# Two-block hybrid layer on one core: forgetting attention summed by even and odd key blocks, the gated recurrence's decays as products, bias table and latent keys made in other stages

## The chip, the cores and the metric

One core of a Trainium2 chip runs the whole program in one launch. The metric is device time in microseconds (us), the median of three runs: 3874.92 before (3865.3 to 3883.36). Engines: TensorE (PE, with its weight loads as PEld), VectorE (DVE), ScalarE (ACT), GpSimd (POOL) and SyncE (SP), which issues all DMAs in order.

## The reference, cut to what matters

Two layers over 2048 tokens of width 1024, all in float32. The first has five branches (spatial gating, forgetting attention, mLSTM, RWKV-7, memory attention), the second a sparse latent attention and a gated recurrence (HGRN2). The change touches three of these:

```python
def forgetting_attention(q, k, v, f_logit, q_g, k_g):   # 4 heads of 64
    q, k = rms_norm(to_heads(q), q_g), rms_norm(to_heads(k), k_g)
    big_f = cumsum(log_sigmoid(f_logit))
    s = einsum("bthd,bshd->bhts", q, k) * scale + big_f[t] - big_f[s]
    return einsum("bhts,bshd->bthd", softmax(causal(s)), v)

def hgrn2(q, f_raw, v, lb):                              # 4 heads, keys and values of 128
    q = silu(q)
    f = lb + (1 - lb) * sigmoid(f_raw)
    k = 1 - f
    # o_t = sum over s <= t of  (q_t . k_s . prod of f over (s, t])  v_s,  chunk by chunk, with a state

def latent_attention(ql, c, bias):                       # c: 128-wide latent keys, rms-normed
    logits = ql @ c.T * scale + rel_bias[bucket(s - t)]  # on the 256 keys picked for each query
    return softmax(logits) @ c
```

## The kernel before

The program is written out flat, and a scheduler puts each engine's instructions in an order by program order and simulated time; on the chip every engine, and SP's queue of DMAs, runs its order as it stands. Pools of tiles are opened on a left and a right side of the memory. A stage on the left (projections: `proj_chunk`, `proj2_chunk`, `gates`) runs beside one on the right (the mixers), and a tile of a new pool waits for the old tiles that lay there. A product in float32 is two PE instructions (a transpose is one), and a projection is three products of single-pass parts (`mm3`, L310 to L316), 24 matmuls for a block of 128 rows and 256 columns.

**Forgetting attention** (`fox_pair`, L793; `attend_pair`, L591). Two heads and 128 queries at a time. For each head the scores of `ns` key blocks go from PE through a DVE copy that keeps the maximum into a tile P (three buffers), ACT takes the exponential in place, and DVE inverts the sum. Then, for both heads together, four 128x128 transposes (two key blocks of two heads) fill a PSUM bank, ACT copies it to PT, and PE sums values into `o`, head 0 into its partitions 0 to 63 and head 1 into 64 to 127, so neighbouring matmuls use different halves of the columns (L616 to L628). At the end one copy, one transpose and two scaled products (L635) give the rows. The "CAM" projections of the first layer come later in program order and fill PE. After the attention its right-hand pools are closed and those of the mixers are opened (L849 onward: `mlstm_setup`, `mem_load`, `sgu_setup`).

**Gated recurrence** (`hgrn_quarter`, L1959), 512 tokens at a time, after projections of 6, 6 and 4 blocks of tokens (`proj2_chunk`, part "hgrn"). The forget gate is stored as exp(-f_raw) (L1401). `hgrn_decays` makes log f with two logarithms on ACT and a subtraction on POOL, and 1 - k with an exponential. Per head, a scan on DVE (L1979) gives the running sum b of log f. The scores within 128 tokens are split by levels, 64, 32, 16, 8, 4, 2, 1 and 0: at level lv the pairs of (key in the first half, query in the second half of a span of 2 lv tokens) are the product of two arrays that carry the decay up to the middle:

```python
nc.gpsimd.tensor_tensor(out=both(e), in0=both(b), in1=ref, op=ALU.subtract)              # L1992
nc.scalar.activation(out=v(e, j), in_=v(e, j), func=ACT.Exp, scale=2.0 * j - 1.0)        # L1994, j = 0, 1
nc.vector.tensor_tensor(out=v(e, 0), in0=v(e, 0), in1=v(kk, 0), op=ALU.mult)             # L1995
nc.vector.tensor_tensor(out=v(e, 1), in0=v(e, 1), in1=v(q, 1), op=ALU.mult)              # L1996
```

Levels 64 to 16 use small matmuls (L2007), the others eight matmuls of 64x64 each (L2018), merged into `near` by a predicated copy (L2019). Every level is made from b, independently of the others. Then exp(b) and exp(b_last - b) give the queries and keys for the state (L2025 to L2032), the keys are transposed, and a loop over four chunks of 128 tokens (L2037 to L2062) loads values hgv (L2041), multiplies scores and values (L2045), adds the state's part (L2046), updates the state (L2049, L2051), norms and gates the rows.

**Latent attention's setup.** While the gates' projection (`gates`, L1439, weights from L298, blocks by fours) runs beside the last quarter, before its third part `dsa_setup` (L1559) makes the bias table: a small matmul gives 4 rows of 512 floats in 4 partitions (gv), and one DMA (L1585) writes each row 128 times to DRAM (gd, 1 MB); four loads with a skewed pattern (L1589) bring `rel`. Before the fourth part `dsa_keys` (L1593) loads, norms and transposes the latent keys in four parts. `attend` (L2237) then runs the sparse attention beside the last projections.

Of the kernel before, what the change touches and what calls it, by code (L numbers as in the profile page):

```python
# [20 lines left out]
T = 2048  # L21
# [9 lines left out]
def _consts():  # L31
# [559 lines left out]
def attend_pair(k, get_s, ns, V, sz, y, bufs=3):  # L591


    nc = k.nc
    L = ns * 128
    o = k.bank("o", 1, 256)
    rden, Ps = [], []
    for h in range(2):
# [16 lines left out]
        rden.append(rd)  # L615
        Ps.append(P)  # L616

    for j0 in range(0, ns, 2):
        n = min(2, ns - j0)
        tp = k.bank("tp")  # L620
        work = [(h, j) for j in range(j0, j0 + n) for h in range(2)]
        for i, (h, j) in enumerate(work):
            k.transpose(tp[:, 128 * i:128 * i + 128], Ps[h][:, 128 * j:128 * j + 128])
        PT = k.wk.tile([128, 512], F32, tag="PT", name="PT", bufs=3)
        k.evict(PT[:, 0:256 * n], tp[:, 0:256 * n], "a")
        for i, (h, j) in enumerate(work):
# [88 lines left out]
def fox_setup(k, q_g, k_g, f_b):  # L715
# [9 lines left out]
    k.fox_fb = k.row(f_b, 4, "fox_fb")  # L725
    k.fox_F = k.const.tile([128, NB, 4, 2], F32R, name="fox_F")
# [635 lines left out]
def proj2_chunk(k, S, slots, w, blocks, part):  # L1362
# [87 lines left out]
def lb_setup(k, lb_logits):  # L1450

    nc = k.nc
    k.lb = k.const.tile([128, 4], F32, name="lb")
# [10 lines left out]
    nc.vector.tensor_tensor(out=k.lb, in0=l[:, 0], in1=m, op=ALU.mult)  # L1464
# [94 lines left out]
def dsa_setup(k, w_uk, w_uv, kv_g, rel_bias):  # L1559
    nc = k.nc  # L1560
    k.w_uk = k.const.tile([128, 4, 128], F32, name="w_uk")
    nc.sync.dma_start(out=k.w_uk, in_=w_uk.rearrange("h d r -> d h r"))
    k.w_uv = k.const.tile([128, 4, 128], F32, name="w_uv")
    nc.sync.dma_start(out=k.w_uv, in_=w_uv.rearrange("h r v -> r h v"))
    k.kv_g = k.row(kv_g, 128, "kv_g")
    k.cT = k.const.tile([128, 2, T], F32R, name="cT")
    k.cM = k.const.tile([128, NB, 128], F32, name="cM")
    k.last64 = k.const.tile([128, 128], BF16, name="last64")
    t = k.wk.tile([128, 128], F32, tag="cn", name="cn", bufs=1)
    nc.sync.dma_start(out=t, in_=k.cd["last64"])  # L1570
    nc.vector.tensor_copy(out=k.last64, in_=t)

    oh = k.wk.tile([32, 511], F32, tag="oh", name="oh", bufs=1)
# [19 lines left out]
def dsa_keys(k, S, part):  # L1593
# [334 lines left out]
def hgrn_setup(k, norm_g):  # L1928
    nc = k.nc
    k.hg_next = []  # L1930
# [4 lines left out]
    k.h_reset = k.const_in("h_reset", [128, 512])  # L1935
# [3 lines left out]
    k.h_mask = k.const.tile([128, 5, 64], U8, name="h_mask")  # L1939
    t = k.wk.tile([128, 320], F32, tag="hgm", name="hgm", bufs=1)  # L1940
    nc.sync.dma_start(out=t, in_=k.cd["h_mask"])
    nc.vector.tensor_copy(out=k.h_mask.rearrange("p l t -> p (l t)"), in_=t)


def hgrn_decays(k, S, h, qt):

    nc = k.nc
    f2, b2 = (k.wk.tile([128, 2, 512], F32, tag="hg" + n, name="hg" + n) for n in ("f", "b"))
    nc.sync.dma_start(out=f2, in_=S["f"][128 * h:128 * h + 256, 512 * qt:512 * qt + 512].rearrange("(h p) t -> p h t", p=128))

    for j in range(2):
        nc.scalar.activation(out=b2[:, j], in_=f2[:, j], func=ACT.Ln, scale=k.lb[:, h + j:h + j + 1], bias=1.0)
# [347 lines left out]
```

## Time and profile before

| | us |
|---|---|
| median of three runs | 3874.92 |
| lowest, highest run | 3865.3, 3883.36 |
| the profiled execution's own time | 3866.28 |
| its span in the profile | 3864.1 |
| PE busy in the span | 3541.2 (92%) |
| PEld, DVE, ACT, POOL busy | 3280.1, 2537.0, 1532.7, 764.6 |

The profile is of one execution. A line like L1994 is the line of the kernel before. In rows of groups, "x192 | 68.7, 412" means 192 instructions, 68.7 us of busy time, 412 ns the mean of one, then the idle time of that engine just before them and who ended it. PE's busy time counts pipelined instructions once where they overlap. PEclk is the granted clock as a share of full speed.

### The profile page before, as it was taken

Reading aid. Unit: us, or ns where it says so; the run is one execution under the profiler, and the core shown is the slowest. Engines: PE = TensorE matmul, PEld = TensorE weight load, DVE = VectorE, ACT = ScalarE, POOL = GpSimd, SP = SyncE. Lnnn points to the kernel's source line nnn. Section 1 sums busy time; section 2 is a strip of 40 time slices with the busy share of each in tenths; the row PEclk is TensorE's granted clock in tenths of the full one; section 3 lists DMA queues with packets and bytes.
Section 4 is the critical chain, followed back from the end, with each engine's and each line's share of the span. In section 5 each row is a group of like instructions: output and inputs, shape, how many; then the busy total and the mean of one; then the engine's idle time right before and its main releaser. Section 6 shows DMA issues by size and latency. Waiting matters only on the chain. (4 is left out here: it accounts for less than half of the span.)

```text
span 3864.1 us, 75038 instructions
## 1 busy us (share of the span) xinstructions
PE 3541.2 (92%) x28525; PEld 3280.1 (85%) x28525; DVE 2537.0 (66%) x7303; ACT 1532.7 (40%) x3257; POOL 764.6 (20%) x686
## 2 busy tenths in 40 slices
PE   6899999999899999789999989889888839899997
PEld 5899989889789999668898989878888838899997
DVE  5477777775734434488655478799777847665675
ACT  3221221222534434444422356566454533443443
POOL 2322222333100000102200000022043423331121
PEclk8999999999999999769899999989999969999998
DMA  8674444445632533446877785774646446653433
GB/s 291 205 224 138 133 157 138 145 144 171 196 120 101 173 130 115 145 141 209 261 247 250 249 263 207 227 238 150 228 161 209 166 115 197 215 187 135 137 124 114
DMA packets 449539, 691.54 MB, mean 179 GB/s; under 512 B 80324, under 2 KB 368526, under 8 KB 410256
## 3 DMA queue, kind: packets, MB, share of 16 engines
q1 hardware_dynamic: 449168, 686.65, 53.9%
q8 instruction: 226, 3.70, 0.4%
q14 instruction: 145, 1.19, 0.1%
HBM read 453.84 MB, written 232.69 MB: 178 GB/s over the span
## 5 line engine op out<-in xcount | busy, mean ns | idle before, releaser
L314 PE MATMUL pj<-whi,slot 128*128 128x256 f32 (+3 forms) x3856 | 1123.8, 292 | 33.1 <-DVE po L178 16.2
L316 PE MATMUL pj<-whi,slot 128*128 128x256 f32 (+3 forms) x3856 | 1119.9, 291 | 2.6 <-DVE slot L271 2.6
L315 PE MATMUL pj<-wlo,slot 128*128 128x256 f32 (+3 forms) x3856 | 1114.6, 289 | 0.8 <-POOL wlo L302 0.8
L314 PEld LDWEIGHTS pj<-whi,slot 128*128 128x128 f32 x3856 | 742.9, 193 | 56.4 <-DVE po L178 16.8
L316 PEld LDWEIGHTS pj<-whi,slot 128*128 128x128 f32 x3856 | 741.4, 192 | 18.9 <-issue 9.0
L315 PEld LDWEIGHTS pj<-wlo,slot 128*128 128x128 f32 x3856 | 742.9, 193 | 14.3 <-issue 7.7
L314 PE MATMUL pj<-slot,whi 128*128 128x256 f32 (+1 forms) x1280 | 385.1, 301 | 33.6 <-DMA slot<-X1T 16.2
L316 PE MATMUL pj<-slot,wlo 128*128 128x256 f32 (+1 forms) x1280 | 381.1, 299 | 0.5 <-DMA wlo<-w8l 0.5
L315 PE MATMUL pj<-slot,whi 128*128 128x256 f32 (+1 forms) x1280 | 380.9, 298 | 0.0
L302 POOL TENSOR_TENSOR wlo<-wraw,whi 128x512 fp32r<-128x512 f32 (+4 forms) x196 | 262.0, 1349 | 596.5 <-ACT whi L301 559.4
L314 PEld LDWEIGHTS pj<-slot,whi 128*128 128x128 f32 x1280 | 255.0, 199 | 43.3 <-issue 27.4
L176 ACT ACTIVATE PT<-tp 128x512 f32<-128x512 f32 (+3 forms) x304 | 157.3, 549 | 270.1 <-PE tp L181 269.7
L315 PEld LDWEIGHTS pj<-slot,whi 128*128 128x128 f32 x1280 | 254.9, 199 | 4.0 <-issue 1.9
L316 PEld LDWEIGHTS pj<-slot,wlo 128*128 128x128 f32 x1280 | 253.9, 199 | 4.6 <-issue 1.3
L1631 ACT ACTIVATE ir<-i 128x512 f32<-128x512 f32 (+2 forms) x304 | 160.5, 543 | 114.8 <-PE i L1629 45.6
L1632 DVE SCALAR_TENSOR_TENSOR sc<-ir,iw,sc 128x512 f32<-128x512 f32 (+2 forms) x266 | 189.3, 712 | 17.0 <-ACT ir L1631 7.4
L301 ACT ACTIVATE whi<-wraw 128x512 fp32r<-128x512 f32 (+4 forms) x196 | 117.7, 619 | 179.8 <-DMA wraw<-in_w_in_dram 109.9
L1629 PE MATMUL i<-ik,iq 128*128 128x512 f32 (+2 forms) x608 | 164.9, 376 | 14.1 <-ACT ir L1631 12.6
L606 DVE TENSOR_SCALAR_CACHE_REDUCE P<-s 128x512 f32<-128x512 f32 (+3 forms) x160 | 94.0, 609 | 125.4 <-PE s L832 45.6
L181 PE MATMUL tp<-c_ident,P 128*128 128x128 f32 x1088 | 166.8, 278 | 2.0 <-DVE fq L809 0.6
L1864 PE MATMUL o<-PT,cM 128*128 128x128 f32 x1088 | 143.9, 277 | 0.7 <-ACT PT L176 0.6
L181 PEld LDWEIGHTS tp<-c_ident,P 128*128 128x128 f32 x1088 | 126.3, 142 | 16.8 <-issue 10.3
(528 smaller groups left out, 7170.5 us busy)
## 6 DMA issues: line engine op xcount, KB each, us to landing
slot<-X1T SPq DMA_DIRECT2D x32, 1024.0 KB, 9.5
wraw<-in_w_in_dram SPq DMA_DIRECT2D x96, 256.0 KB, 3.8
X1T<-slot SPq DMA_DIRECT2D x16, 1024.0 KB, 8.2
xT<-slot SPq DMA_DIRECT2D x11, 1024.0 KB, 7.0
slot<-xT SPq DMA_DIRECT2D x11, 1024.0 KB, 5.4
yr<-Y SPq DMA_DIRECT2D x16, 640.0 KB, 6.8
sD<-po SPq DMA_DIRECT2D x64, 132.0 KB, 2.6
xt<-in_x_dram SPq DMA_DIRECT2D x16, 512.0 KB, 5.3
```

The costliest lines, as they stand in the source:

```text
L176: self.nc.scalar.activation(out=out, in_=in_, func=ACT.Copy)
L181: self.nc.tensor.matmul(out=out, lhsT=in_, rhs=self.ident[0:in_.shape[0], 0:in_.shape[0]], is_transpose=True, start=True, stop=True)
L301: nc.scalar.activation(out=h, in_=raw, func=ACT.Copy)
L302: nc.gpsimd.tensor_tensor(out=lo[:, g:g + m, 0:n], in0=raw, in1=h.bitcast(F32), op=ALU.subtract)
L314: k.nc.tensor.matmul(out=out, lhsT=ah, rhs=bh, start=(i == 0), stop=False)
L315: k.nc.tensor.matmul(out=out, lhsT=ah, rhs=bl, start=False, stop=False)
L316: k.nc.tensor.matmul(out=out, lhsT=al, rhs=bh, start=False, stop=(i == m - 1))
L606: nc.vector.tensor_scalar(out=P[:, s0:s0 + n], in0=p[:, 0:n], scalar1=1.0, scalar2=None, op0=ALU.mult, op1=ALU.max, accum_out=mx[:, nch:nc ...
L1629: nc.tensor.matmul(out=p[:, 0:n], lhsT=iq[:, h], rhs=k.ik[:, i, s0:s0 + n], start=(i == 0), stop=(i == 1))
L1631: nc.scalar.activation(out=r, in_=p[:, 0:n], func=ACT.Relu, scale=0.125)
L1632: nc.vector.scalar_tensor_tensor(out=o, in0=r, scalar=k.iw[:, qb, h:h + 1], op0=ALU.mult, op1=ALU.add, in1=o if h else k.dsa_tiny[:, s0:s0 ...
L1864: nc.tensor.matmul(out=o[:, 0:128], lhsT=k.cM[:, j0 + j], rhs=PT[:, 128 * j:128 * j + 128], start=(j0 + j == 0), stop=(j0 + j == ns - 1))
```

## The change

1. `attend_pair` finishes one head before the next: it transposes four key blocks of one head, sums even key blocks into partitions 0 to 63 and odd ones into 64 to 127, and adds the two halves with a matmul against two stacked identities (`fox_fold`).
2. The forget gate is stored as f itself (a tanh and one multiply-add). `hgrn_quarter` works on two heads at a time and uses only products: K and Q start as 1 - f and q f, and after the scores of each level K's first halves and Q's second halves are multiplied in place by the neighbouring span's decay T, whose products go from level to level. No logarithm, exponential, scan or subtraction is left, and POOL has no part in the scores. The levels run from 1 up to 64.
3. The bias table is made by `rel_setup` after `mem_setup` in the first layer: the four rows go to DRAM once, and for each head a load spreads its row over 128 partitions and a store writes them.
4. The latent keys are made after the second chunk of the recurrence's projections, in a pool below that stage's, with banks of the projections; their squares are summed by ACT.

The diff, cut:

```diff
@@ attend_pair
-    o = k.bank("o", 1, 256)
+    o = k.bank("o", 1)
...
-    for j0 in range(0, ns, 2):
-        n = min(2, ns - j0)
-        tp = k.bank("tp")
-        work = [(h, j) for j in range(j0, j0 + n) for h in range(2)]
-        for i, (h, j) in enumerate(work):
-            k.transpose(tp[:, 128 * i:128 * i + 128], Ps[h][:, 128 * j:128 * j + 128])
...
+        c = slice(128 * h, 128 * h + 128)
+        for j0 in range(0, ns, 4):
+            n = min(4, ns - j0)
+            tp = k.bank("tp")
+            for j in range(n):
+                k.transpose(tp[:, 128 * j:128 * j + 128], P[:, 128 * (j0 + j):128 * (j0 + j) + 128])
+            PT = k.wk.tile([128, 512], F32, tag="PT", name="PT", bufs=3)
+            k.evict(PT[:, 0:128 * n], tp[:, 0:128 * n], "a")
+            for j in range(n):
+                e = 64 * (j % 2)
+                nc.tensor.matmul(out=o[e:e + 64, c], lhsT=V(j0 + j, h), rhs=PT[:, 128 * j:128 * j + 128],
+                                 start=(j0 + j < 2), stop=(j0 + j >= ns - 2))
+        m = 64 * min(2, ns)
+        ot = k.wk.tile([128, 128], F32, tag="ot", name="ot", bufs=1)
+        k.evict(ot[0:m], o[0:m, c])
+        d = slice(64 * h, 64 * h + 64)
+        tp = o[:, 256 + 64 * h:320 + 64 * h]
+        nc.tensor.matmul(out=tp, lhsT=ot[0:m], rhs=k.fox_fold[0:m], start=True, stop=True)
+        nc.vector.scalar_tensor_tensor(out=y[:, d], in0=tp, scalar=rd, in1=sz[:, d], op0=ALU.mult, op1=ALU.mult)
@@ proj2_chunk, forget
-        nc.vector.tensor_scalar(out=o, in0=p, scalar1=-43.0, scalar2=None, op0=ALU.max)
-        nc.scalar.activation(out=o, in_=o, func=ACT.Exp, scale=-1.0)
+        nc.scalar.activation(out=o, in_=p, func=ACT.Tanh, scale=0.5)
+        nc.vector.tensor_scalar(out=o, in0=o, scalar1=k.lb[:, 1, c:c + 1], scalar2=k.lb[:, 0, c:c + 1],
+                                op0=ALU.mult, op1=ALU.add)
@@ dsa_setup becomes rel_setup, keys_setup, dsa_setup
-    gd = k.dr.tile([4, 128, 512], F32, name="gd")
-    nc.sync.dma_start(out=gd, in_=g.unsqueeze(1).to_broadcast([4, 128, 512]))
+    row = k.dr.tile([4, 512], F32, name="gr")
+    nc.sync.dma_start(out=row, in_=g)
+    k.gd = k.dr.tile([4, 128, 512], F32, name="gd")
+    for h in range(4):
+        t = room("gb")[:, 0:512]
+        nc.sync.dma_start(out=t, in_=bc(row[h]))
+        nc.sync.dma_start(out=k.gd[h], in_=t)
@@ dsa_keys
-    c = k.wk.tile([128, 4, 128], F32, tag="cw", name="cw", bufs=1)
-    nc.sync.dma_start(out=c, in_=slab(S["cw"], part, 0, 128, 4))
-    r = k.head_rms(c, 4, 128, "dk")
+    nc.sync.dma_start(out=cm, in_=slab(S["cw"], part, 0, 128, 4))
+    ss = k.sm.tile([128, 4], F32, tag="dkss", name="dkss")
+    for j in range(4):
+        sq = k.wk.tile([128, 128], BF16, tag="dkq", name="dkq", bufs=1)
+        nc.scalar.activation(out=sq, in_=cm[:, j], func=ACT.Square, accum_out=ss[:, j:j + 1])
...
@@ hgrn_quarter (all of the part per head is replaced)
+    for g in range(2):
+        F, q = wt("f"), wt("q")
+        r = slice(256 * g, 256 * g + 256)
+        for x, n in ((F, "f"), (q, "hq")):
+            nc.sync.dma_start(out=x, in_=S[n][r, t0:t0 + 512].rearrange("(h p) t -> p h t", p=128))
+        K_, Q = wt("k"), wt("Q", 4)
+        nc.vector.tensor_scalar(out=flat(K_), in0=flat(F), scalar1=-1.0, scalar2=1.0, op0=ALU.mult, op1=ALU.add)
+        two.append((F, q, K_, Q, wt("T"), k.wk.tile([128, 2, 256], F32, tag="hgC", name="hgC")))
+
+    def scores(x, y):
+        p = k.bank("h", 3)
+        for h in range(2):
+            for s in range(0, 512, 64):
+                r, o = s % 128, 256 * h + 64 * (s // 128)
+                nc.tensor.matmul(out=p[r:r + 64, o:o + 64], lhsT=x[:, h, s:s + 64], rhs=y[:, h, s:s + 64],
+                                 start=True, stop=True)
+        return p
+
+    for F, q, K_, Q, T_, near in two:
+        p = scores(K_, q)
+        nc.vector.tensor_tensor(out=c4(flat(near)), in0=c4(p), in1=k.h_diag.unsqueeze(1).to_broadcast([128, 8, 64]),
+                                op=ALU.mult)
+        nc.vector.tensor_tensor(out=flat(Q), in0=flat(q), in1=flat(F), op=ALU.mult)
+    o = 0
+    for i, n in enumerate((1, 2, 4, 8, 16, 32, 64)):
+        m = 1024 // n
+        for g, (F, q, K_, Q, T_, near) in enumerate(two):
+            T = (flat(F) if n == 1 else flat(T_)[:, o:o + m]).rearrange("p (n j) -> p n j", j=2)
+            if n < 64:
+                p = scores(K_, Q)
+                nc.vector.copy_predicated(out=c4(flat(near)), mask=k.h_mask[:, i].unsqueeze(1).to_broadcast([128, 8, 64]),
+                                          data=c4(p))
+            else:
...
+            halves = lambda x, j: flat(x).rearrange("p (n j i) -> p n j i", j=2, i=n)[:, :, j]
+            for x, j in ((K_, 0), (Q, 1)):
+                nc.vector.tensor_tensor(out=halves(x, j), in0=halves(x, j), op=ALU.mult,
+                                        in1=T[:, :, 1 - j:2 - j].to_broadcast([128, m // 2, n]))
+            to = last[:, g].rearrange("p h c -> p (h c)") if n == 64 else flat(T_)[:, o + m * (n > 1):][:, 0:m // 2]
+            nc.vector.tensor_tensor(out=to, in0=T[:, :, 0], in1=T[:, :, 1], op=ALU.mult)
+        o += m * (n > 1)
@@ body
             mem_setup(k, L("mem"), L("mem_norm_g"), L("mem_w_kv"), L("mem_k_g"))
+            rel_setup(k, w["rel_bias_2"])
...
+        base = k.open(const=1)
...
                 proj2_chunk(k, S2, get_slots(k, X1T, blocks), L("w_in_2"), blocks, "hgrn")
+                if q == 0:
+                    with k.using(base):
+                        keys_setup(k, w["kv_norm_g_2"][0])
...
+                if q == 3:
+                    for part in range(4):
+                        dsa_keys(k, S2, part, k.pj_tag, k.pj)
...
-                if p == 3:
-                    for part in range(4):
-                        dsa_keys(k, S2, part)
```

## Rows read from the trace of the kernel before

**Rows 1.** Busy time by stage; columns in the first line.
```profile
core 0: us, PE busy (x) PEld busy (x) DVE busy (x) ACT busy (x) POOL busy (x), PEclk, DMA share, GB/s
1009.00:1586.00 577.00, 570.60 (x4771) 515.35 (x4771) 250.12 (x898) 243.43 (x487) 2.99 (x5) 0.99 0.37 127
...
2815.00:3110.00 295.00, 256.16 (x3160) 243.26 (x3158) 228.41 (x492) 156.59 (x332) 132.80 (x98) 0.96 0.49 167
3110.00:3145.00 35.00, 18.32 (x130) 15.70 (x130) 24.40 (x61) 14.65 (x29) 9.36 (x7) 0.71 0.75 217
3145.00:3183.00 38.00, 0.66 (x4) 0.42 (x4) 5.60 (x15) 0.60 (x1) 0.00 (x0) 0.54 0.30 44
3183.00:3313.00 130.00, 115.32 (x1113) 108.48 (x1114) 99.49 (x267) 44.45 (x105) 47.61 (x39) 0.95 0.64 192
3350.00:3700.00 350.00, 342.70 (x2747) 334.42 (x2746) 221.51 (x479) 155.01 (x277) 77.88 (x41) 1.00 0.44 153
```

**Rows 2.** The same view for the middle of the stall.
```profile
3150.00:3180.00 30.00, 0.00 (x0) 0.00 (x0) 0.64 (x5) 0.00 (x0) 0.00 (x0) 0.50 0.32 48
```

**Rows 3.** Waits from 3138 to 3190: us in total, times, longest.
```profile
PE h L2045 <- DMA hgv<-s2hv: 35.9, 1, 35.9
```

**Rows 4.** SP's queue in order of time: start, length of the issue.
```profile
3138.38 0.82 SPq L1585 DMA_DIRECT2D gd<-gv  x1
3140.71 13.48 SPq L2041 DMA_DIRECT2D hgv<-s2hv  x1
...
3182.90 1.28 SPq L1589 DMA_DIRECT2D rel<-gd  x3
```

**Rows 5.** DMA issues: count, size of one, us to landing.
```profile
slot<-X1T SPq DMA_DIRECT2D x32, 1024.0 KB, 9.5
```

**Rows 6.** Busy time of lines L2018 and L2007 alone, 2815 to 3313.
```profile
2815.00:3313.00 498.00, 54.45 (x1280) 45.71 (x1280) 0.91 0.53 168
...
2815.00:3313.00 498.00, 21.17 (x896) 18.60 (x896) 0.91 0.53 168
```

**Rows 7.** Groups of instructions by line and shape, 2815 to 3313.
```profile
L1992 POOL TENSOR_TENSOR hge<-hgb 128x512 f32<-128x512 f32 x96 | 116.6, 1239 | 102.8 <-PE h L2007 57.0 <-PE h L2018 17.2 <-DVE hgK L178 10.3
...
L1994 ACT ACTIVATE hge<-hge 128x256 f32<-128x256 f32 x192 | 68.7, 412 | 30.7 <-POOL hge L1992 30.1
...
L1996 DVE TENSOR_TENSOR hge<-hge,hgq 128x256 f32<-128x256 f32 x96 | 59.9, 624 | 0.0
L1995 DVE TENSOR_TENSOR hge<-hge,hgf 128x256 f32<-128x256 f32 x96 | 56.8, 592 | 8.9 <-ACT hge L1994 8.3
...
L2019 DVE COPY_PREDICATED hgC<-h_mask,h 128x256 f32<-128x256 uint8 x80 | 35.4, 442 | 14.6 <-PE h L2018 10.1 <-ACT hgC L2011 1.9
...
L1979 DVE TENSOR_TENSOR_SCAN hgb<-c_h_reset,hgb 128x512 f32<-128x512 f32 x16 | 24.4, 1544 | 9.2 <-ACT hgf L1955 9.2
```

**Rows 8.** Tiles hge and hgf: ns min/median/max, first and last start.
```profile
L1996 DVE TENSOR_TENSOR hge<-hge,hgq x96: 349/415/1496, 2841.7 to 3267.5; 128x256 f32<-128x256 f32 x96
...
L2032 DVE TENSOR_TENSOR hgf<-hgeb,hgf x16: 677/681/1730, 2855.7 to 3274.7; 128x512 f32<-128x512 f32 x16
```

**Rows 9.** Groups by line and shape, 1009 to 1586: the sums of values.
```profile
L627 PE MATMUL o<-PT,fv 128*64 128x128 f32 x1088 | 79.8, 282 | 2.1 <-ACT PT L176 2.1
```

**Rows 10.** SP's queue where the forgetting attention ends.
```profile
1586.70 0.37 SPq L838 DMA_DIRECT2D Y<-fy  x1
...
1587.68 2.16 SPq L855 DMA_DIRECT2D conv_w<-in_mlstm_conv_w_dram  x4
```

**Rows 11.** Busy time by stretch around that end, columns as in rows 1.
```profile
1586.00:1595.00 9.00, 9.00 (x76) 8.83 (x74) 2.50 (x10) 1.16 (x3) 0.00 (x0) 1.00 0.51 68
1595.00:1625.00 30.00, 8.30 (x29) 5.09 (x29) 21.10 (x72) 17.87 (x34) 6.93 (x6) 0.56 0.57 169
```

**Rows 12.** PE in order of time: start, length; projections in a row.
```profile
2913.15 0.28 PE L316 MATMUL pj<-whi,slot 128*128 128x256 f32 x1
2913.27 0.28 PE L314 MATMUL pj<-whi,slot 128*128 128x256 f32 x1
```

More of the change, by code (lines that the diff above doesn't have):

```diff
@@ L725, in fox_setup @@
     k.fox_fb = k.row(f_b, 4, "fox_fb")
+    k.fox_fold = k.const.tile([128, 64], F32, name="fox_fold")
+    nc.vector.tensor_tensor(out=k.fox_fold, in0=k.ident[:, 0:64], in1=k.ident[:, 64:128], op=ALU.add)
     k.fox_F = k.const.tile([128, NB, 4, 2], F32R, name="fox_F")
@@ L1452, in lb_setup @@
     nc = k.nc
-    k.lb = k.const.tile([128, 4], F32, name="lb")
+    k.lb = k.const.tile([128, 2, 4], F32, name="lb")
     l = k.sm.tile([128, 2, 4], F32, tag="lbl", name="lbl")
@@ L1463, in lb_setup @@
     nc.vector.reciprocal(out=m, in_=m)
-    nc.vector.tensor_tensor(out=k.lb, in0=l[:, 0], in1=m, op=ALU.mult)
+    nc.vector.tensor_tensor(out=m, in0=l[:, 0], in1=m, op=ALU.mult)
+    for i, c in enumerate((0.5, -0.5)):
+        nc.vector.tensor_scalar(out=k.lb[:, i], in0=m, scalar1=c, scalar2=0.5, op0=ALU.mult, op1=ALU.add)
 LN_EPS = 1e-5
@@ L1556, in dsa_pick_load, with rel_setup @@
     nc.vector.tensor_scalar(out=w, in0=w, scalar1=8 ** -0.5, scalar2=None, op0=ALU.mult)
-def dsa_setup(k, w_uk, w_uv, kv_g, rel_bias):
+def rel_setup(k, rel_bias):
     nc = k.nc
[L1561 to L1573, printed above, removed]
+    room = lambda n: k.wk.tile([128, D], F32, tag="xt", name=n, bufs=2)
+    oh = room("oh")[0:32, 0:511]
     nc.sync.dma_start(out=oh, in_=k.cd["bucket"])
@@ L1934, in hgrn_setup, with hgrn_quarter @@
     nc.vector.memset(k.hg_s, 0.0)
[L1935 removed]
     k.hg_a = k.const.tile([128, 4, 4, 128], F32, name="hg_a")
     nc.gpsimd.memset(k.hg_a, 0.0)
[L1939 to L1940 removed]
+    k.h_mask = k.const.tile([128, 6, 64], U8, name="h_mask")
+    k.h_diag = k.const.tile([128, 64], F32, name="h_diag")
+    t = k.wk.tile([128, 448], F32, tag="hgm", name="hgm", bufs=1)
     nc.sync.dma_start(out=t, in_=k.cd["h_mask"])
[L1942 to L1952, printed above, removed]
[L1953 to L1959 removed]
+    nc.vector.tensor_copy(out=k.h_diag, in_=t[:, 0:64])
+    nc.vector.tensor_copy(out=k.h_mask.rearrange("p l t -> p (l t)"), in_=t[:, 64:448])
+def hgrn_quarter(k, S, Y2, qt):
     nc = k.nc
@@ new lines, in hgrn_quarter @@
+    last = k.sm.tile([128, 2, 2, 4], F32, tag="hgl", name="hgl")
+    flat = lambda x: x.rearrange("p h t -> p (h t)")
+    wt = lambda n, bufs=2: k.wk.tile([128, 2, 512], F32, tag="hg" + n, name="hg" + n, bufs=bufs)
+    c4 = lambda x: x.rearrange("p (c t) -> p c t", t=64)
+    two = []
+    for g in range(2):
[6 more added lines that the diff above has]
+        two.append((F, q, K_, Q, wt("T"), k.wk.tile([128, 2, 256], F32, tag="hgC", name="hgC")))
@@ new lines, in hgrn_quarter @@
+    o = 0
[9 more added lines that the diff above has]
+                p = k.bank("h", 3)
+                for h in range(2):
+                    for s in range(0, 512, 128):
+                        d = 256 * h + s // 2
+                        nc.tensor.matmul(out=p[0:64, d:d + 64], lhsT=K_[:, h, s:s + 64], rhs=Q[:, h, s + 64:s + 128],
+                                         start=True, stop=True)
+                for h in range(2):
+                    nc.scalar.activation(out=A[0:64, :, 2 * g + h, 64:128], in_=c4(p[0:64, 256 * h:256 * h + 256]),
+                                         func=ACT.Copy)
+                    for r in (0, 64):
+                        nc.scalar.activation(out=A[r:r + 64, :, 2 * g + h, r:r + 64], in_=c4(near[r:r + 64, h]),
+                                             func=ACT.Copy)
+            halves = lambda x, j: flat(x).rearrange("p (n j i) -> p n j i", j=2, i=n)[:, :, j]
[5 more added lines that the diff above has]
+        o += m * (n > 1)
@@ L2037, in hgrn_quarter @@
+    for g, (F, q, K_, Q, T_, near) in enumerate(two):
+        for h in range(2):
+            p = k.bank("h", 3)
+            for c in range(4):
+                k.transpose(p[:, 128 * c:128 * c + 128], K_[:, h, 128 * c:128 * c + 128])
+            k.evict(kT[:, :, 2 * g + h], p.rearrange("p (c t) -> p c t", c=4))
     St = k.hg_s
```

130 lines of the change are left out of this document (32 added, 98 removed).

## The prediction

> **What bounds the kernel now.** I read the busy time by stage first. TensorE (PE) is the engine that limits most of the span: in the forgetting attention's stage (1009 to 1586 us) it is busy 570.6 of 577 us, in the latent attention's (3350 to 3700) 342.7 of 350 [rows 1]. The stage of the recurrence, 2815 to 3313, is the exception: its four rows add up to 498 us with 390.5 us of PE, so 107.5 us idle, and DVE at 358 us. The reader should see two different things in these rows. From 3145 to 3183 PE has 0.66 us of work, and inside that, from 3150 to 3180, no engine but DVE does anything, and DVE 0.64 us [rows 1, 2]: everything waits. In the 295 us before, PE is at 87% with DVE at 77%, POOL at 45% and ACT at 53%: a PE that waits for its helpers.
>
> Next I asked who ends the wait. PE's first instruction after it (L2045, the chunk's output) waited 35.9 us for the load of hgv [rows 3]. The queue of SP shows why that load was late: `gd<-gv`, the bias table of L1585, is issued at 3138.38, the hgv load behind it at 3140.71 needs 13.48 us only to be issued, and the loads of `rel` from gd, which wait for its end, come at 3182.90 [rows 4]. So 1 MB (4 x 128 x 512 floats) took 44.5 us, some 24 GB/s, where another 1 MB, a slot of X1T, lands in 9.5 us [rows 5].
>
> **The change, part by part.** All sums are against the profiled execution: span 3864.1, its own time 3866.28 us. The median of the runs shown, 3874.92, lies 8.6 us above it; I add that at the end.
>
> *Bias table.* The table leaves the recurrence's stage and is made where the first block's memory keys are made, beside the forgetting attention. The stall of 38 us with 0.66 us of work in it goes: **-37 us**. What is late next there is the load of the gate weights, which waited behind the same transfer and goes with it. The new way is one write of four rows, then per head a load spread over 128 partitions and a store from them, 2 MB in all; at the price of a slot, 9.5 us per MB [rows 5], 19 us of DMA in a stage whose DMA share is 0.37 [rows 1]. It adds 12 issues to SP's queue there (three small loads, the row write, eight pieces), most of which wait for the one before; behind them in that queue are the stores of projected rows and the loads of weights. Two matmuls and three small DVE instructions come with it. I take **+2 us**; the bounds are 0 and the whole old stall again (+37), if the queue stands still while PE has no other work.
> The Trainium skill (DMA: Bandwidth & Descriptors, Rules for kernel authors) says that a DMA whose outermost dimension counts fewer than 16 runs on at most so many DMA engines. The old table has 4 there, and the share of 0.32 in the stall, other loads included, agrees with four of sixteen [rows 2]. By that rule the new pieces, 128 outermost, take a quarter of 44.5 us per MB, 11 us, and the sum stays the same.
>
> *Recurrence on PE.* Before, 896 + 1280 score instructions take 21.2 + 54.5 us of PE [rows 6]. After, a pair of heads has seven levels of 16 matmuls and one of 8, 120, two instructions each: 240, and 1920 in eight pairs. At 54.45 / 1280 = 42.5 ns that is 81.7 us: **+6 us**, on the path where PE is full.
>
> *Recurrence on DVE, ACT, POOL.* The levels' exponentials (L1994, 68.7 us of ACT) and subtractions (L1992, 116.6 us of POOL) go [rows 7]. On DVE four lines alone go with 59.9 + 56.8 + 35.4 + 24.4 = 176.5 us [rows 7], and five smaller instructions of 256 elements or more per head, 16 x 5 x 0.415 = 33 us at least: 209 us. New, per pair of heads: a multiply of 256 elements is 0.415 us, of 512 0.681 [rows 8], so 1024 is 1.2; predicated copies of 512 out of PSUM 0.71 by 0.442 for 256 [rows 7] and the same slope. K and Q 2.4 (K has one input and may be cheaper), the diagonal 0.7, six levels of 0.71 + 2 x 0.68, a seventh of 1.36, and the products of decays, 0.68 + 0.415 + five of about 0.2: 18.5 us, 148 in eight pairs. DVE falls by 60 us if multiplies run at their median. They ran at a mean of 0.624 against a median of 0.415 [rows 7, 8]; if that excess stayed, the new sum would be 148 x 1.5 = 222 and DVE would gain nothing.
> What this is worth I read from another stage: in the latent attention PE is at 97.9% with DVE at 63% [rows 1]. DVE here would come to (358 - 60) / 460 = 65%. Without the stall the stage is 460 us with 390 of PE, 85%; with 396 us at 95% it takes 417: **-43 us** (95 and not 98, since a level's in-place products must wait for the scores that read them, and the last quarter has only the gates beside it). Bounds: no better share, +6; 98% and the slow stretch of 3110 to 3145 (granted clock 0.71, between its two levels) at full clock, -65.
>
> *The forget gate* trades a DVE and an ACT instruction for the same two in the other order: 0. *Latent keys* move from the gates to the time of the third chunk of projections: loads, squares, transposes and all. On DVE a part is three instructions of 512 elements at 0.681 and twelve tiny ones below 0.415: 7 us, 28 in four; covered by projections there, and 0 as long as DVE stays near two thirds. If that cover is gone, they cost PE one part's wait, 7 us. The load of kv_g and the four loads of keys come earlier in SP's queue, ahead of the last chunk's weights: 0 to +3.
>
> *Forgetting attention.* PE's work rises a little: with an odd number of key blocks the last one has no partner in the other half of the columns, 2 x 8 x 2 matmuls, 64 instructions that run alone, at 79.8 / 1088 = 73 ns [rows 9] of lost overlap each, 4.7 us; 64 folds of two instructions at 42.5 ns, 5.4 us, replace 32 transposes, some 3 us more. PE is 99% busy, so **+8 us**. Against that, a head's P is free after its own sums, no longer after both heads'; with three buffers the next softmax can run on. The projections fill PE either way, so the stage gets no shorter, but its own chain ends earlier. That matters at its end: the attention's last rows leave at 1586.70, the mixers' first setup load at 1587.68, projections fill PE until 1595, and then PE has 8.3 us of work in 30 [rows 10, 11]. If the chain ends 10 us or more earlier the setup lies under the projections. Of the 21.7 idle us I take 13: **-13 us**, bounds 0 and -22.
>
> Sum: -37 + 2 + 6 - 49 + 8 - 13 = **-83 us** (the +6 is inside the 417 above, so -43 is written as 6 - 49): 3783 for such an execution, **3792** for the median.
>
> **Rivals.**
> 1. *Only the stall closes.* The chain of in-place products keeps PE at 85%: 3874.9 - 37 + 2 + 6 + 8 - 13 = 3841. For: every level now needs PE, then DVE, then PE on one tile, where before all levels came from one array. Against: two pairs of heads alternate, and ACT and POOL drop out of the chain. 0.18.
> 2. *The table's new place jams.* Its pieces hold SP's queue while PE at 99% has no slack; 30 us come back: 3822. Against: the pieces are spread over 128 partitions. 0.07.
> 3. *Slower: the levels run one after the other.* Place: the second and the last quarter, where a score waits in PE's order behind a projected block of 24 matmuls, 0.12 us apart [rows 12], 2.9 us, then 32 of its own, 1.4, then DVE 2.4: 6.7 us a round, 14 rounds, 94 us and 10 around them, where DVE now spends 209 / 4 = 52. Twice 52 us more, less the 37 of the stall, with +2 + 6 + 8 - 13 for the rest: 3945. It decides from a round of 5 us on, where two quarters eat the stall's gain. 0.06.
> 4. *The forgetting attention shortens itself.* Its PE is busy 99%, but weight loads fill only 515.35 / 577 = 89%, and 95.5% in the latent attention [rows 1]; brought to that share it would take 38 us less: 3792 + 5 - 38 = 3759, in place of + 8 - 13. The Trainium skill (Trainium Kernel Development and Optimization, Performance Expectations) calls matmul busy time a bad metric and weight-load share a good one; its rule gives this rival. [...] 0.10.
> 5. *The stall isn't the table's*: then nothing but small terms is left, 3870. The queue's order [rows 4] speaks against it. 0.02.
>
> **How the numbers follow.** The forecast, 3765 to 3818, has 0.57; its own range stands for the bounds of the share (93 to 97%) and of the attention's end. The range to 8 in 10 takes in rivals 1, 2 and 4: **3747 to 3848**. 0.5% is 19 us, about what a measurement of this kernel can tell from no change: faster by more needs little beyond the stall, 0.57 + 0.10 + 0.07 + 0.15 of rival 1 = 0.89; same 0.05 (the rest of 1, and 5); slower 0.06.
>
> **What would show it.** Right: no stretch of 30 us without PE work after the third chunk; `rel` loads right after the table's time of need with no wait for gd; POOL almost empty between 2815 and the end of the recurrence, DVE there below 70% and PE above 92%; the latent attention starts some 80 us earlier; the mixers' setup loads are issued before the last projection of their stage ends. Wrong: predicated copies or products that wait for PE in each level, PE idle ended by DVE products of the recurrence, a wait for the table's row or pieces in the early stage, or DVE multiplies still at 0.6 us. The forecast falls if PE's share in the recurrence stays at 85%, or if the first 1600 us get longer.

## The result and the profile after

The changed kernel takes 3755.39 us (median of four runs, 3742.49 to 3765.99) against 3871.89 (four, one more than stood above, 3865.3 to 3883.36): a ratio of 0.9695, interval 0.9656 to 0.9734, some 116 us less. 3792 was forecast, with 3747 to 3848 as range. The profiled execution took 3754.19 us, its span 3752.3, 111.8 below that of before.

Where they went, by the busy time of PE between the same events in both traces (first softmax copy of the forgetting attention, first index score, last instruction of the picks, first maximum of the latent attention; the picks are the choice of 256 keys for each query from the index scores):

| stretch | before: us, PE busy, idle | after: us, PE busy, idle | forecast | measured |
|---|---|---|---|---|
| up to the forgetting attention | 1006.0, 942.2, 63.8 | 1008.6, 943.4, 65.2 | 0 | +2.6 |
| attention and mixers | 1149.9, 1085.0, 64.9 | 1142.1, 1092.4, 49.7 | -3 | -7.8 |
| index scores and picks | 659.7, 609.4, 50.3 | 647.6, 598.1, 49.5 | 0 | -12.1 |
| recurrence | 496.1, 388.6, 107.5 | 403.7, 373.3, 30.4 | -80 | -92.4 |
| latent attention | 552.4, 516.0, 36.4 | 550.3, 514.8, 35.6 | 0 | -2.1 |

PE's idle time falls by 92 us and its busy time by 19, with nearly the same number of instructions (28365 for 28525). The busy time by stretch of the kernel after (columns as in rows 1; a line number in a profile line is that of the kernel whose trace it comes from):

```profile
core 0: us, PE busy (x) PEld busy (x) DVE busy (x) ACT busy (x) POOL busy (x), PEclk, DMA share, GB/s
1009.00:1556.00 547.00, 540.78 (x4474) 484.68 (x4475) 250.92 (x903) 243.85 (x507) 3.62 (x5) 0.98 0.36 124
1556.00:1595.00 39.00, 23.94 (x167) 20.96 (x167) 22.21 (x89) 15.46 (x33) 0.95 (x1) 0.75 0.72 216
1595.00:1700.00 105.00, 97.08 (x655) 84.44 (x655) 82.69 (x267) 46.37 (x119) 8.53 (x10) 0.84 0.43 135
2798.00:3160.00 362.00, 346.17 (x4070) 334.98 (x4069) 244.46 (x605) 62.79 (x145) 50.40 (x40) 1.00 0.65 211
3160.00:3201.00 41.00, 26.46 (x133) 25.21 (x131) 4.07 (x7) 8.29 (x15) 12.25 (x10) 0.83 0.85 271
```

The recurrence runs from 2798 to 3160 with PE at 95.6% and the granted clock at 1.00, its higher level of 2.4 GHz; the stall of [rows 1, 2] is gone. The last 41 us, with no recurrence left, have a hole of their own: 14.5 us idle, 11.1 of them one wait for the load of dq, the latent attention's first queries. The attention leaves its last rows at 1556 in place of 1586, with weight loads at 484.68 / 547 = 88.6%, close to the 89.3% of before. The same two stretches in the kernel before:

```profile
1595.00:1700.00 105.00, 68.85 (x282) 49.45 (x281) 87.77 (x273) 51.39 (x119) 17.71 (x16) 0.55 0.56 185
2815.00:3311.00 496.00, 389.04 (x4398) 366.45 (x4396) 355.99 (x820) 215.41 (x462) 189.78 (x144) 0.91 0.53 168
```

Between 1595 and 1700 PE did 282 instructions at a mean granted clock of 0.55, near the lower level of 1.2 GHz; now it does 655 at 0.84. The table's pieces in SP's queue (start, length of the issue), and what each needs to land (count, size, us):

```profile
1063.69 0.31 SPq L1577 DMA_DIRECT2D gr<-gv  x1
1064.09 0.38 SPq L837 DMA_DIRECT2D Y<-fy  x1
1064.52 0.92 SPq L817 DMA_DIRECT2D fz<-sB  x1
1065.53 0.71 SPq L757 DMA_DIRECT2D fx_q<-sB  x1
1068.41 0.81 SPq L1581 DMA_DIRECT2D gb<-gr  x2
...
1077.99 1.04 SPq L1582 DMA_DIRECT2D gd<-gb  x2
```
```profile
gb<-gr SPq DMA_DIRECT2D x4, 256.0 KB, 3.7
gd<-gb SPq DMA_DIRECT2D x4, 256.0 KB, 3.1
```

Row, four loads and four stores, 2 MB, are through some 18 us after the first issue; 1 MB took 44.5 before [rows 4], and the issues between them are short.

### The profile page after: what moved, and what is told of

Same layout as the page of the kernel before. It is cut to its first block, busy times and chain, and to the rows that moved or that the text cites. A ratio compares the mean times of both kernels' runs of the same rounds, so it can differ in the third digit from the quotient of the medians.

```text
span 3752.3 us, 74094 instructions
## 1 busy us (share of the span) xinstructions
PE 3521.8 (94%) x28365; PEld 3272.7 (87%) x28365; DVE 2430.2 (65%) x7159; ACT 1393.1 (37%) x3007; POOL 624.0 (17%) x582
## 5 line engine op out<-in xcount | busy, mean ns | idle before, releaser
L315 PEld LDWEIGHTS pj<-whi,slot 128*128 128x128 f32 x3856 | 744.4, 193 | 18.6 <-issue 9.4
L313 PEld LDWEIGHTS pj<-slot,whi 128*128 128x128 f32 x1280 | 250.9, 196 | 38.5 <-issue 16.8
L314 PEld LDWEIGHTS pj<-slot,whi 128*128 128x128 f32 x1280 | 250.9, 196 | 3.3 <-issue 1.6
L1753 ACT ACTIVATE dst<-sc,dste 128x256 bf16<-128x256 f32 (+5 forms) x126 | 120.0, 952 | 57.1 <-DVE dste L1720 50.3
```

Of the source, the lines that this page charges most:

```text
L313: k.nc.tensor.matmul(out=out, lhsT=ah, rhs=bh, start=(i == 0), stop=False)
L314: k.nc.tensor.matmul(out=out, lhsT=ah, rhs=bl, start=False, stop=False)
L315: k.nc.tensor.matmul(out=out, lhsT=al, rhs=bh, start=False, stop=(i == m - 1))
L1753: nc.scalar.activation(out=trash2[:, 0:LA], in_=scs[i][:, L - LA:L], func=ACT.Sign, scale=-1.0, bias=ti, accum_out=ca[:, i:i + 1])
```

## The experiments

The theory after the two traces: three independent gains (the table's transfer, the recurrence's products, the attention's order), and two moves (table and latent keys to other stages) that are worth nothing by themselves. The rivals: the moves matter; or the gains are given back where another part isn't there. One caution for single profiles: the first stretch, the same work in all these kernels but for the order, ended between 1001 and 1017 us, so differences below some 10 us are not read.

**The table: place or shape?** Edit: the kernel before, with the table made in the first layer and spread (e1); and in its old place, but spread (e2):

```diff
@@ e1: body (rel_setup as in the change; the table's part of dsa_setup goes)
             mem_setup(k, L("mem"), L("mem_norm_g"), L("mem_w_kv"), L("mem_k_g"))
+            rel_setup(k, w["rel_bias_2"])
...
@@ e2: dsa_setup
+    row = k.dr.tile([4, 512], F32, name="gr")
+    nc.sync.dma_start(out=row, in_=g)
     gd = k.dr.tile([4, 128, 512], F32, name="gd")
-    nc.sync.dma_start(out=gd, in_=g.unsqueeze(1).to_broadcast([4, 128, 512]))
+    for h in range(4):
+        t = k.wk.tile([128, 512], F32, tag="gb", name="gb", bufs=2)
+        nc.sync.dma_start(out=t, in_=bc(row[h]))
+        nc.sync.dma_start(out=gd[h], in_=t)
```


> The kernel before with the bias table alone made in the first layer, spread over 128 partitions. If the transfer of the table is what stops the recurrence's stage, the stretch without PE work near 3145 goes, 38 us, and the pieces cost 0 to 3 us in their new place: 3835 to 3840 us against 3872. If another wait (the gate weights, the loads of latent keys) stands behind it, half of it stays: 3850. If the table was never the cause: 3870.

> The kernel before with the table written from 128 partitions, but in its old place. Row, loads and stores took 1063.7 to about 1084 us in the changed kernel, some 20 us, in place of 44.5. If the four partitions of the old write are what makes it slow, PE's stop shrinks from 38 us to about 15: 3848 to 3852 us. If any chain of transfers at that place of the queue costs the same, no change: 3872. If the shape is all of it: 3836.

Measured: e1 3843.22 us, 0.9935 (0.9916 to 0.9954), 25 us less; e2 3819.6 us, 0.9887 (0.986 to 0.9913), 49 us less. So the shape is enough: without a move the gain is larger. In e1 the recurrence got only 18.6 us shorter, in e2 41 us (the stage in e1, then in e2):

```profile
2815.00:3292.50 477.50, 401.19 (x4466) 380.11 (x4465) 346.64 (x826) 224.33 (x471) 188.47 (x144) 0.92 0.53 174
```
```profile
2808.20:3263.00 454.80, 387.39 (x4394) 364.27 (x4394) 354.97 (x825) 215.28 (x462) 189.76 (x144) 0.94 0.57 185
```

PE's idle time there falls from 107.5 us to 76.3 in e1 and 67.4 in e2. The waits of e1 from 3100 to 3200 show a part of what is left (us in total, times, longest):

```profile
PE h L2056 <- DMA hgv<-s2hv: 20.6, 2, 13.7
```

The wait of [rows 3] is still there, 13.7 us long; from 3140 to 3160 the DMA engines were full (share 1.03). But waiting is the smaller part of what lies between e1 and e2: their spans differ by 28.6 us (3842.8 and 3814.2), of which 5.7 are idle time of PE and 22.9 busy time (3556.8 and 3533.9), for the same work. Why PE took longer over it in e1 is not shown.

The other way round, the changed kernel with the old write in the new place (e7):

```diff
@@ rel_setup
-    row = k.dr.tile([4, 512], F32, name="gr")
-    nc.sync.dma_start(out=row, in_=g)
...
+    nc.sync.dma_start(out=k.gd, in_=g.unsqueeze(1).to_broadcast([4, 128, 512]))
```


> The changed kernel with the table still made in the first layer, but written as before, in one transfer from four partitions. It should again take about 44 us. If a slow transfer hurts only where PE has nothing else to do, the attention's stage covers it: 3753 to 3760 us. If it stops the queue there too, PE idles for 20 to 38 us near 1080 and the time is 3775 to 3792.

Measured: 3792.84 us, 0.9822 (0.9803 to 0.9842), against the changed kernel's ratio of 0.9695 (and 0.9712 below) 43 to 49 us more. Its busy time by stretch, SP's queue and two waits from 1060 to 1115:

```profile
1060.00:1070.00 10.00, 10.00 (x74) 8.49 (x72) 2.49 (x8) 2.88 (x6) 0.00 (x0) 1.00 0.23 26
1070.00:1107.00 37.00, 5.83 (x31) 5.20 (x30) 4.30 (x20) 2.37 (x4) 0.00 (x0) 0.59 0.29 52
1107.00:1150.00 43.00, 43.00 (x310) 38.94 (x309) 16.47 (x59) 15.74 (x33) 0.00 (x0) 0.96 0.42 149
```
```profile
1055.81 0.76 SPq L1577 DMA_DIRECT2D gd<-gv  x1
1056.67 14.79 SPq L837 DMA_DIRECT2D Y<-fy  x1
1071.51 10.13 SPq L817 DMA_DIRECT2D fz<-sB  x1
1081.75 10.19 SPq L757 DMA_DIRECT2D fx_q<-sB  x1
```
```profile
ACT fs_q L203 <- DMA fx_q<-sB: 35.4, 1, 35.4
...
PE tp L180 <- ACT PT L175: 29.8, 1, 29.8
```

The whole stall is back, in a stage where PE is 99% busy without it and full of projections: the next three issues take 10 to 15 us each where they take less than 1 above, so the load of the next queries is 35 us late; the attention's chain stops, one transpose waits in PE's fixed order, and the projections stand behind it. The Trainium skill (DMA: Bandwidth & Descriptors, Rules for kernel authors) has the rule of the outermost dimension for this; the share of 0.29 in the stall agrees with four engines of sixteen (0.25), other transfers included.

**The recurrence's products** alone on the kernel before (e4: `forget`, `lb_setup`, `hgrn_setup` and `hgrn_quarter` of the change with the masks they use, nothing else):

```diff
-def hgrn_decays(k, S, h, qt):
...
-def hgrn_quarter(k, S, Y2, qt, more):
...
+def hgrn_quarter(k, S, Y2, qt):
...
```


> The kernel before with the recurrence's products (and the gate stored as f) alone; table and latent keys stay where they were. The recurrence to the latent attention's start took 496 us before and 402 after; less 38 of the stall that is 56 us for the products: 3812 to 3820 us, with the stall of some 38 us still in the trace. If part of the 56 comes from the latent keys' earlier place or from the stall's going: 3830 to 3845. If the products are worth only what PE's share of 95% would give (49 less 6): 3829.

Measured: 3808.47 us, 0.9851 (0.9821 to 0.9881), 60 us less, with the stall still in it (6.15 us of PE work from 3115 to 3155), now as a wait for gate weights:

```profile
PE s L313 <- ACT whi L300: 41.7, 2, 35.0
```

So the products are worth 60 us without help from the other parts. What they run at, by line and shape in the kernel after:

```profile
L1994 PE MATMUL h<-hgQ,hgk 128*64 128x64 f32 x1536 | 53.7, 225 | 11.2 <-DVE hgQ L2027 8.9 <-issue 1.4 <-DVE last L1606 0.5
...
L2027 DVE TENSOR_TENSOR hgQ<-hgQ,hgT 128x512 f32<-128x512 f32 x48 | 37.0, 772 | 0.0
L2010 DVE COPY_PREDICATED hgC<-h_mask,h 128x512 f32<-128x512 uint8 x48 | 35.3, 735 | 13.3 <-PE h L1994 13.3
L2027 DVE TENSOR_TENSOR hgk<-hgk,hgT 128x512 f32<-128x512 f32 x48 | 33.6, 700 | 3.5 <-PE h L2017 3.3
...
L2017 PE MATMUL h<-hgQ,hgk 128*64 128x64 f32 x128 | 9.2, 225 | 0.0
...
L1994 PE MATMUL h<-hgq,hgk 128*64 128x64 f32 x256 | 8.8, 224 | 0.0
```

PE waited for a level's products 8.9 us in all; the 1920 scores take 71.7 us.

Does POOL's silence have a part in that? The changed kernel with idle subtractions on POOL (e9; they are added work, and no output depends on them):

```diff
@@ hgrn_quarter, in each level and pair
+            idle = k.wk.tile([128, 512], F32, tag="hgx", name="hgx", bufs=1)
+            nc.gpsimd.tensor_tensor(out=idle, in0=k.hg_g, in1=k.hg_g, op=ALU.subtract)
```


> The changed kernel with an idle subtraction on POOL (128x512, result unused) ahead of the products of each level and pair of heads, 56 of about 1.24 us. In the kernel before, with POOL busy 45% of the recurrence, DVE's products took a mean of 592 to 624 ns against a median of 415; in the changed kernel, POOL at a tenth, those of 512 elements take 676 to 820 ns. If POOL's work is what stretches DVE's, single products go up to 1.2 us and more beside POOL's, DVE gains 20 to 40 us of busy time, and the kernel loses 3 to 20 us. If not, DVE's means stay and the time stays: 0 to 3 us.

Measured: 3774.37 us, 0.976 (0.9732 to 0.9788), 20 us above the changed kernel measured beside it (e12 below). As no instruction uses their result, all 56 ran in the first 101 us of the stage, so one can compare that stretch, first with and then without them (groups, then busy time):

```profile
L2026 POOL TENSOR_TENSOR hgx<-hg_g 128x512 f32<-128x512 f32 x56 | 70.4, 1257 | 12.2 <-PE i L1811 8.3
...
L2029 DVE TENSOR_TENSOR hgQ<-hgQ,hgT 128x512 f32<-128x512 f32 x12 | 18.3, 1524 | 0.0
...
L2029 DVE TENSOR_TENSOR hgk<-hgk,hgT 128x512 f32<-128x512 f32 x12 | 11.5, 955 | 0.0
L2010 DVE COPY_PREDICATED hgC<-h_mask,h 128x512 f32<-128x512 uint8 x12 | 8.7, 727 | 0.0
```
```profile
2809.00:2910.00 101.00, 88.58 (x1029) 85.62 (x1028) 90.75 (x158) 12.71 (x30) 77.22 (x61) 0.93 0.48 161
```
```profile
L2010 DVE COPY_PREDICATED hgC<-h_mask,h 128x512 f32<-128x512 uint8 x12 | 8.8, 736 | 3.0 <-PE h L1994 3.0
L2027 DVE TENSOR_TENSOR hgQ<-hgQ,hgT 128x512 f32<-128x512 f32 x12 | 8.2, 685 | 0.0
L2027 DVE TENSOR_TENSOR hgk<-hgk,hgT 128x512 f32<-128x512 f32 x12 | 8.2, 681 | 1.2 <-PE h L2017 1.1
```
```profile
2798.00:2899.00 101.00, 99.58 (x1165) 97.22 (x1164) 68.11 (x174) 15.01 (x36) 10.29 (x8) 1.00 0.57 193
```

With POOL at 76% the products of two tiles in SBUF go from 685 to 1524 ns and from 681 to 955; the predicated copies, whose data come from PSUM, stay at 730. PE loses 11 us in 101. The Trainium skill (SBUF — State Buffer, section "SBUF: two separate sides") says that a DVE instruction with two SBUF inputs and a POOL instruction that reads SBUF lock each other out; products and copies agree with it. Over the whole stage (419.0 us, against 403.7 in the changed kernel) PE's wait for a level's products grows from the 8.9 us above to 16.9, and 2.9 more are put down to POOL:

```profile
PE h L1994 <- DVE hgQ L2029: 16.9, 16, 3.8
...
PE h L2048 <- POOL hgx L2026: 2.9, 1, 2.9
```

So 70 us of POOL cost this kernel about 20. That POOL's silence is a part of e4's 60 us is an inference from this: POOL was busy for 190 us of the stage before and for 62 in e4.

**The forgetting attention** of the change, whole, on the kernel before (e3), and the changed kernel with that of before (e5):

```diff
@@ e3: attend_pair, fox_setup
-    o = k.bank("o", 1, 256)
+    o = k.bank("o", 1)
...
+        nc.tensor.matmul(out=tp, lhsT=ot[0:m], rhs=k.fox_fold[0:m], start=True, stop=True)
@@ e5: attend_pair, fox_setup
-    o = k.bank("o", 1)
+    o = k.bank("o", 1, 256)
...
-        nc.tensor.matmul(out=tp, lhsT=ot[0:m], rhs=k.fox_fold[0:m], start=True, stop=True)
```


> The kernel before with the forgetting attention alone changed. By the two traces the attention's chain ends 33 us earlier, and by 2798 us some 17 us of it are left, the rest is handed back as projections that the stage did not get to: 3853 to 3857 us. If that is chance of the order of instructions and all is handed back: 3866 to 3872. If the stage keeps the 33 us: 3839.

> The changed kernel with the forgetting attention as it was. Put alone on the kernel before, that part gained 14 us; its trace was 29 us ahead when the picks ended and 17 us behind in the recurrence, where the table's stall is. If a part's gain simply adds: 3755 + 14 = 3769 us. If the stall took 17 us of it back and without the stall all of it shows: 3784. If nothing is left of it in the changed kernel: 3755.

Measured: e3 3854.35 us, 0.9963 (0.9947 to 0.9979), 14 us less than before; e5 3782.18 us, 0.9771 (0.9738 to 0.9803), 23 to 29 us above the changed kernel by the ratios (0.9695, and 0.9712 below). In both pairs the picks end about 30 us earlier with it, counted from the attention's start (1781.6 against 1809.6 us, 1789.7 against 1820.9). On the kernel before, the recurrence then takes 17.5 us longer again, 13 of it PE work that had been done during the picks; in the changed kernel 5. So the gain is there on both, and the recurrence of the kernel before takes more than half of it back. The stretch from 1593 in e5 shows what the early end removes:

```profile
1593.00:1700.00 107.00, 71.82 (x339) 52.96 (x337) 84.50 (x262) 47.77 (x108) 17.90 (x16) 0.62 0.58 185
```

The mixers' own 1317 PE instructions (tiles m and q, summed over their lines) take 260.0 us before and 258.2 in e5, but 236.8 after and 238.4 in e3: the same work, 22 us less. What differs is what is left to run between them: of each of the three matmuls of a projection 409 fall into this stage before and 416 in e5, but 564 after and 582 in e3, and the granted clock over the stage is 0.87 and 0.86 against 0.92 and 0.91. That the clock makes the difference is read from these two pairs; no run changes it alone. The stage and two of its lines, before and after:

```profile
1586.40:2155.90 569.50, 512.59 (x3571) 450.48 (x3570) 373.03 (x1114) 205.03 (x510) 74.68 (x66) 0.87 0.69 224
...
L316 PE MATMUL pj<-whi,slot 128*128 128x256 f32 x409 | 121.5, 298 | 0.0
...
L666 PE MATMUL q<-mem_k,qT 64*128 64x256 f32 x128 | 31.8, 483 | 2.1 <-DVE my L699 1.4 <-ACT qT L660 0.7
```
```profile
1556.00:2150.70 594.70, 551.58 (x4046) 496.06 (x4045) 380.15 (x1144) 211.94 (x532) 75.28 (x66) 0.92 0.72 234
...
L315 PE MATMUL pj<-whi,slot 128*128 128x256 f32 x564 | 166.5, 295 | 0.0
...
L663 PE MATMUL q<-mem_k,qT 64*128 64x256 f32 x128 | 29.5, 425 | 0.7 <-ACT qT L657 0.6
```

Is it the order of the heads or the two halves of the columns? The changed kernel, each head in its own half (e8):

```diff
@@ attend_pair (no folds; copy, transpose and scaling at the end as before)
-        c = slice(128 * h, 128 * h + 128)
+        c = slice(64 * h, 64 * h + 64)
...
-                e = 64 * (j % 2)
-                nc.tensor.matmul(out=o[e:e + 64, c], lhsT=V(j0 + j, h), rhs=PT[:, 128 * j:128 * j + 128],
-                                 start=(j0 + j < 2), stop=(j0 + j >= ns - 2))
...
+                nc.tensor.matmul(out=o[c, 0:128], lhsT=V(j0 + j, h), rhs=PT[:, 128 * j:128 * j + 128],
+                                 start=(j0 + j == 0), stop=(j0 + j == ns - 1))
...
```


> The changed kernel with the forgetting attention head by head, but each head summed in its own half of the columns, as before, with no even and odd blocks and no folds. If the gain there is that a head's P comes free earlier, it stays, less 13 us of folds: 3745 to 3755 us. If alternating halves matter, neighbouring sums no longer overlap: at 73 ns for each of 1088 instructions 79 us more of PE, most of it on the path: 3800 to 3835.

Measured: 3802.5 us, 0.9844 (0.9823 to 0.9866), 20 us slower than e5 measured beside it, so worse than the old attention. The sums of values, e8 and after:

```profile
L624 PE MATMUL o<-PT,fv 128*64 128x128 f32 x1087 | 138.6, 280 | 1.0 <-ACT PT L175 1.0
```
```profile
L624 PE MATMUL o<-PT,fv 128*64 128x128 f32 x1088 | 82.0, 281 | 0.3 <-ACT PT L175 0.2 <-DVE fy L633 0.2
```

The mean of one is the same, the busy time is not: 56.6 us more, 52 ns for each instruction that no longer overlaps its neighbour. So even and odd blocks are what makes head by head affordable.

**The moves.** Latent keys back in the gates' time (e6), the table back there, spread (e10), the kernel before with the edits of e2, e3 and e4 together and both old places (e11), and the changed kernel again, beside e9 to e11 (e12):

```diff
@@ e6: body
-                if q == 3:
-                    for part in range(4):
-                        dsa_keys(k, S2, part, k.pj_tag, k.pj)
...
+                if p == 3:
+                    for part in range(4):
+                        dsa_keys(k, S2, part, "tp")
@@ e10: body, attend_setup
-            rel_setup(k, w["rel_bias_2"])
...
+    rel_setup(k, w["rel_bias_2"])
```


> The changed kernel with the latent keys made in the gates' time again, ahead of their fourth part. The table's move alone left a wait of 13.7 us for the values behind the loads of gate weights, and gained 25 us where 37 were expected. If the latent keys' loads and their DVE and ACT work there are what was late next, it returns: 3767 to 3772 us. If covered work was only moved: 3755. If the keys' new place is a burden on the last quarter: 3745.

> The changed kernel with the table made in the gates' time, where the kernel before makes it, but spread over 128 partitions. If only the shape of the write counts, it is the changed kernel's time within 5 us. If the place in the first layer costs what the two single steps differ by (3843 against 3820 us), it gains up to 24 us. If the twelve small transfers at the old place hold up the gates' loads, it loses 10 to 20 us.

> The kernel before with three parts alone: the forgetting attention, the recurrence's products, and the table's write spread over 128 partitions in its old place; latent keys stay in the gates' time. By the single runs the gains of 14 to 27, 60 and 49 us add to 123 to 136 less what the parts share: if neither move matters, the changed kernel's time within 5 us; if the old places are the better ones, 10 to 24 us below it; if the latent keys' earlier place is worth something, 5 to 10 above it.

> The changed kernel itself, on the chip and in the rounds of the three others, to compare them with: 0.9695 of the kernel before, between 0.966 and 0.973.

Measured: e6 3765.67 us, 0.9762 (0.9741 to 0.9784), its five runs from 3739.05 to 3776.59; e10 3745.51 us, 0.9691 (0.9668 to 0.9714); e11 3748.39 us, 0.9694 (0.9666 to 0.9721); e12 3753.99 us, 0.9712 (0.9689 to 0.9736). e10 and e11 lie 5 to 9 us below the changed kernel, inside the intervals: three parts with one changed transfer give all of the gain, and neither move adds any that these runs can tell. e6's ratio is half a per cent above e12's and the intervals do not overlap, but it was taken on another chip with runs that spread over 1%, and its trace is that of the fastest (3739.05), with no loss to see. Since e11 keeps the latent keys in that same place and isn't slower, whether the place costs anything is left open.

## Why the prediction came out as it did

The direction and the range held, and so did the causes given for the table and the recurrence; of the attention's mechanism one half failed. The size did not hold: 83 us were forecast, 116 measured, and each of the three large terms was too small. The time misses the forecast's own 3765 to 3818; it lies in the wider range because rival 4 had stretched that downwards, and rival 4's mechanism did not come, so this is in part luck.

*The table, -37.* The cause (the transfer, and SP's queue behind it) was right. I priced what is late next at nothing, "goes with it"; alone in the new place the table left a wait of 13.7 us and gave 25 (e1), alone in the old place it gave 49 (e2), and the old write costs 43 to 49 when it comes back (e7). The bound on the new place, "the whole old stall again (+37), if the queue stands still while PE has no other work", had the wrong condition: e7 pays all of it in a stage full of other work, which stands in PE's order behind what waits. The prediction's estimate of 11 us per MB makes 2.8 us for a piece; they took 3.1 and 3.7. Their cost to the path, +2, can't be told from 0.

*The recurrence, +6 and -49.* Alone the products gave 60 us (e4). The scores did not cost 6 more but 4 less (71.7 us for 1920, 37 ns each, against 75.6 [rows 6]). DVE's new work was forecast at 148 us (its terms add up to 19.0 us for a pair of heads, not 18.5, so to 152); the lines of the new part take 155. Their products' mean is 700 to 772 ns with a median near 680: most of the old excess of a half is gone. DVE falls from 356.0 to 248.5 us in the stage, by 108 and not by 60, because the lines that went had taken 245 us and not 209, and the norms' small instructions that stayed (tiles rs_t, rs_y, r and ss) fell from 64 us to 38. PE's share came as forecast, 95.6%, and 92.5% with the hole at the end. The step that failed is "with 396 us at 95%": the stage has 373 us of PE work, not 396, although 64 projections more fell into it. The old durations carried the granted clock of 0.91 in them; the same 128 sums took 28.3 us before and 24.8 after, at 0.98:

```profile
L2045 PE MATMUL h<-hgv,hg_a 128*128 128x128 f32 x128 | 28.3, 307 | 44.6 <-DMA hgv<-s2hv 42.1 <-DVE rs_y L192 2.4
```
```profile
L2046 PE MATMUL h<-hgv,hg_a 128*128 128x128 f32 x128 | 24.8, 275 | 1.1 <-DMA hgv<-s2hv 1.1
```

I had the clock only as an outer bound.

*The attention, +8 and -13.* On PE it cost more: 128 fold instructions 22.3 us where I took 42.5 ns each, less 8.9 for the old transposes, and 2.2 for lone sums, 15.6 in all. PE's idle time from the attention to the index scores fell by 15.2, close to the 13. But "The projections fill PE either way, so the stage gets no shorter" failed: the stage ended 30 us earlier (1556 for 1586) with 136 fewer of each projection matmul in it (617 and 481); with these behind it, in the mixers' stage, the granted clock there was higher and the mixers' instructions took 22 us less, behind the hole of [rows 11]. Over attention, mixers and picks together -3 were forecast, the table's +2 included, and -19.9 measured; e3 and e5 show the 22 us alike.

*The latent keys, 0.* Not to be told from 0. They did not run beside the third chunk of projections, as I had it: their squares and products ran from 2521 to 2559 us, in the picks' stage, and only the transposes at 2912.

*The rivals.* Rival 1 (share stays at 85%) did not come. Rival 2's jam exists, but belongs to the shape, not the place (e7). Rival 3: PE waited 8.9 us in all for products, no rounds of 5 us. Rival 4 gave 3759, nearer to the 3755 than my 3792, but not by its mechanism: the weight loads' share in the attention's stage stayed at 88.6%, and the gain came in the stage behind it. Rival 5 is refuted by e2 and e7.

## What to carry to other kernels

A hole in PE's work is paid twice where, as here from 1595 to 1700, the granted clock stays low behind it: price it by the instructions done at each clock, not by the idle time alone. A filler in a fixed order need not hide a late transfer: in e7 one transpose that waited stopped everything behind it. Test a changed transfer in its old place before moving it: here the shape was all, and the move nothing.

## What was not expected

One slow transfer makes the *issues* behind it slow: with 1 MB from four partitions under way, three issues took 14.79, 10.13 and 10.19 us in e7, against 0.38, 0.92 and 0.71 in the changed kernel. Idle POOL instructions whose results nobody uses cost 20 us, in good part through DVE's slower products. And neighbouring sums in the same half of PE's columns cost 52 ns more each than in alternating halves, at the same recorded duration of 280 ns: busy time shows it, the mean does not.
